# A decoder layer on one core: entries of the SwiGLU layers with other token operands first, and their tensor operations on VectorE alone

## The chip, the core and the metric

The kernel runs on one core of one Trainium2 chip. The metric is the device time of one execution in microseconds (us), and the numbers compared are medians over runs. The core has a matmul engine (TensorE, "PE" in the profile), a vector engine (VectorE, "DVE"), an activation engine (ScalarE, "ACT"), GpSimd ("POOL"), and SyncE ("SP"), which here issues the DMA transfers. Every engine works through its own queue in the order in which its instructions were emitted.

## The reference

One layer of a hybrid decoder trunk, for 1024 tokens of width 1024 in float32:

```python
x = x + 1/2 * SwiGLU_1(RMSNorm(x))
x = x + W_out [ DilatedAttn(heads 0..7) || Retention(heads 0..3) ]
x = x + CrossAttn(RMSNorm(x), RMSNorm(mem))   # 4 heads, 256 memory tokens
x = x + 1/2 * SwiGLU_2(RMSNorm(x))
final RMSNorm
```

A SwiGLU is `silu(x @ Wg) * (x @ Wu) @ Wout` with a hidden width of 2816, and its weights stand in DRAM as float32.

## The kernel before

Each float32 operand of a large matmul is written as a high part (`whi`, `hi...`, rounded by ACT) and a low part (`wlo`, `lo...`, the rest, subtracted by DVE or POOL), and three matmuls high x high, high x low and low x high stand for one. `split` does this for weights: a copy on ACT, L215, then a subtraction, L217, in one of four pairs of buffers.

**The SwiGLU's first half** is `ffn_in`. It goes over the hidden columns in 11 groups (p = 0 to 10). A group computes its gate and up columns by seven products instead of eight (a Strassen scheme on 2x2 blocks: gate and up by the two halves of the 1024 features, and these by the two halves of the 1024 tokens); a product multiplies one of seven token operands with one of seven weight operands. The token operands B11, T1, T2, B21, T3, B22, T4 are made once for a SwiGLU by `make_t`: `minus` (L427) makes differences of normed and transposed tokens, `parts` makes the high part on ACT (L417) and the low part on DVE or POOL (L419), in two halves. The weight operands W[1] to W[7] are made anew in each group: four loads `raw` (`load_raw`, L222), the sums s1 to s4 (`comb`, L497; s1 and s2 and s4 stand in one `hn` buffer, s3 in a `raw` buffer), and a `split` each. W[5] is the split of s1, W[6] of s2, W[7] of s3, W[3] of s4; W[1], W[2] and W[4] are splits of loads. A product is 24 matmuls of 512 columns (L522). In each group the products follow as 1 (B11), 5 (T1), 6 (T2), 2 (B21), 7 (T3), 3 (B22), 4 (T4).

Behind the products: three copies from PSUM on ACT (L533), three additions on DVE (L536), two silu on ACT (L539), then `h2` (L568), `e1` (L551), `h1` (L572), which reads T4's product from PSUM, and `e2`, `e3`, `e4` (L551, halves of 128x512). `h1`, `e1` to `e4` and `h2` are the operands of the second half `ffn_out`; four stores put them in DRAM. Also in each group but the first, `w_sums` (L471) loads 256 rows of the second half's weights, makes four differences of 128x512, and stores them; the last group does this twice.

**The order of all engines** comes from a planner, `Flow.run`: every operation is a node with a duration by a formula, dependences and buffers; the planner places one node after another at its planned time and writes each engine's instructions in that order. An operation on two SBUF tensors may go on DVE or POOL, and takes the engine with the earlier planned end, where `n.bias` is added first; `fl.bias` is empty in the kernel before. Once written, the order on an engine is fixed, and an instruction whose input is late holds all that stand behind it there.

**Around the SwiGLUs.** The first stage makes the keys and values of `mem` in eight blocks j (matmuls L256 to L258, weights `w_ckv`). In block j one tile of 128 rows of x is loaded, normed (the square on ACT L350, L352 on POOL, L353 on DVE) and, one block later, transposed by eight matmuls (L300) into the raw tokens of `make_t`. The eighth tile is transposed after the last block, and then the first SwiGLU starts. The second SwiGLU starts behind the cross attention's output, which is two sweeps (`sweep`) over four halves; in the last one the eight tiles of x come out one after another, are added (L1353), normed and transposed. The buffers for token operands are opened in two lots: T_EARLY (B11, T1, T2) and T_LATE (B21, T3, B22, T4). Before the second SwiGLU, `to_ffn2` closes the cross attention's buffers behind that sweep and opens both lots.

Of the kernel before, what the change touches and what calls it, by code (L numbers as in the profile page):

```python
# [152 lines left out]
def kernel(ctx: ExitStack, tc: tile.TileContext, x, mem,  # L153
# [246 lines left out]
    def make_t(R, done, early, late):  # L402

        def q(j, c):
            return [R[j, c, h] for h in range(2)]
# [4 lines left out]
        def parts(name, src, deps, give=None):  # L410
            out = []
            for h in range(2):
                ts = slice(h * 256, h * 256 + 256)
# [3 lines left out]
                a = N("ACT", cost_act(1024), lambda v=v, ts=ts: act.activation(TT[name][0][:, :, ts], v(), AF.Copy),  # L417
                      deps=deps[h] + [early if name in T_EARLY else late])
                out.append(N(("DVE", "POOL"), (cost_dve(1024), cost_pool(1024)), lambda e, v=v, ts=ts: two[e].tensor_tensor(  # L419
                    TT[name][1][:, :, ts], v(), f32(TT[name][0][:, :, ts]), op=OP.subtract), deps=[a],  # L420
                    give=[src[h]] if give else []))
# [4 lines left out]
        def minus(dst, a, b, deps):
            return [[N(("DVE", "POOL"), (cost_dve(1024), cost_pool(1024)), lambda e, h=h: two[e].tensor_tensor(  # L427
                dst[h].v, a[h].v, b[h].v, op=OP.subtract), deps=deps[h])] for h in range(2)]
# [53 lines left out]
    def ffn_in(wi, hids, wo, wts):  # L482
        stored = {}
        for p in range(NF // 2):
# [2 lines left out]
            if p == NK - 1:  # L487
                w_sums(wo, wts, p, stored)
            raws = {}
            for u, j in ((0, 0), (1, 0), (1, 1), (0, 1)):  # L490
                raws[u, j] = load_raw(rows(wi, j * 512, u * DFF + 2 * p * P, 4, 256), 4)
            (a11, l11), (a21, l21), (a22, l22), (a12, l12) = (raws[k] for k in ((0, 0), (1, 0), (1, 1), (0, 1)))
            sm = Hold(s_hb)
# [3 lines left out]
                         lambda e: two[e].tensor_tensor(dst.v, a.v, b.v, op=op), deps=deps, need=need, give=give)  # L497
# [34 lines left out]
            def copy(dst, b, deps):  # L532
                return N("ACT", cost_act(S), lambda: act.activation(dst.v, flat(b), AF.Copy), deps=deps, need=[dst])  # L533
# [17 lines left out]
                return N(("DVE", "POOL"), (cost_dve(512), cost_pool(512)), lambda e: two[e].tensor_tensor(  # L551
                    o[0](o[1]), a[0](a[1]), b[0](b[1]), op=op), deps=deps, need=need)
# [1 line left out]
            m1 = prod(1, x, "B11", True)
            a = copy(ta, x, [m1])
            z = Hold(pairs)
            m5 = prod(5, z, "T1", True)
            d = copy(td, z, [m5])
            m6 = prod(6, x, "T2", False, [a])
            b_ = copy(tb, x, [m6])  # L560
            y = Hold(pairs)
            m2 = prod(2, y, "B21", True)
            g1 = silu(ta, [add(ta, y, [m2, a], [y])])
            m7 = prod(7, x, "T3", False, [b_])
            u2 = add(td, x, [m7, d])
            m3 = prod(3, z, "B22", False, [d])
            g2 = silu(tb, [add(tb, z, [m3, b_], [z])])
# [139 lines left out]
    mp = open_pool(mctx, "memp")  # L710
# [28 lines left out]
    g1 = load_gain(norm_ffn1[0])  # L739
    R = raw_quarters()  # L740
    rdone = {}
    for j in range(8):
# [17 lines left out]
        kv_stored.append(dma(256, lambda kv=kv, j=j: sp.dma_start(  # L760
            kvs[j * 256:j * 256 + 256].rearrange("(i p) m -> p i m", p=P), kv.v), deps=[c], give=[kv]))
        hb, sc = norm_scale(lambda x_=x_: x_.v, [xl], g1, None, [x_])

        def later(j=j, hb=hb, sc=sc):
            b = Hold(pairs)
            tr = transposes(lambda k: hb.v[:, k * P:(k + 1) * P], [sc], b, give=[hb])
            rdone[j] = to_raw(R, tr, b, j)
        Later.add(1, later)
# [781 lines left out]
```

## Time and profile before

| | |
|---|---|
| median of three runs | 2161.68 us (2161.47 to 2163.49) |
| profiled execution, its own time | 2164.8 us |
| span from first to last instruction | 2163.0 us |
| mean granted TensorE clock | 0.984 |
| first stage | 0 to 75.6 us |
| first SwiGLU, first half | 75.62 to 509.55 us |
| second SwiGLU, first half | 1503.29 to 1941.76 us |

How to read the rows that are shown further on. A row of the timeline has the start in us, the time taken in us, the engine, the line, the operation, what it writes and reads, and the number of instructions that the row joins; in brackets stand the idle time of the engine ahead of it and the instruction that ended it. A row of the table by stretches has the stretch, its length, then the busy time of PE, PE's weight loads, DVE, ACT and POOL, then the granted TensorE clock, the DMA share and GB/s. The chain is the work that ended last, followed back from the end.

### The profile page before, as it was taken

The page shows a single profiled execution, that of the slowest core. Times are in us where ns is not written, and L with a number is a line of the kernel's source. Part 1 is how long each engine was busy: PE and PEld are TensorE (multiplying, and loading weights), DVE is VectorE, ACT ScalarE, POOL GpSimd, SP SyncE. Part 2 cuts the span into 40 slices and gives each one's busy share as a digit, 9 for nine tenths or more (in the row PEclk, how much of TensorE's full clock was granted, in tenths as well). Part 3 has the DMA queues.
Part 4 walks back from the last instruction along what each step waited for, and adds up shares of the span by engine and source line. Part 5 has one row for each costly group of instructions (what it writes and reads, how often), then busy time and mean ns, then how long its engine had stood idle before and what let it go on. Part 6 is the DMA issues. An engine that isn't in the chain of part 4 may idle for free.

```text
span 2163.0 us, 25267 instructions
## 1 busy us (share of the span) xinstructions
PE 2084.8 (96%) x9854; PEld 1724.0 (80%) x9854; DVE 1170.8 (54%) x1351; ACT 808.6 (37%) x1138; POOL 491.5 (23%) x341
## 2 busy tenths in 40 slices
PE   7899999999999999998999999998899999999997
PEld 7678888888888788887677788886688888888886
DVE  6956556565447420304896334525855656474464
ACT  5523323234335211114777423304332323333342
POOL 2533342340003100201220001003533233230031
PEclk9999999999999999998999999998999999999999
DMA  8344435457666542226743911112253544558554
GB/s 299 92 161 152 165 132 175 161 205 259 212 194 214 196 115 88 90 106 188 217 120 113 338 40 49 49 49 98 81 185 138 175 159 152 185 187 290 193 196 148
DMA packets 205991, 344.08 MB, mean 159 GB/s; under 512 B 12464, under 2 KB 100656, under 8 KB 205616
## 3 DMA queue, kind: packets, MB, share of 16 engines
q1 hardware_dynamic: 205872, 342.48, 46.9%
q8 instruction: 77, 1.26, 0.2%
q14 instruction: 42, 0.34, 0.0%
HBM read 239.14 MB, written 103.28 MB: 158 GB/s over the span
## 4 chain that ended last, share of the span: by engine, by line
PE 89%; DVE 5%; DMA 2%; issue 1%; ACT 1%; POOL 1%; SPq 0%; POOLq 0%; DVEq 0%; ACTq 0%
PE banks L522 37%; PE banks L630 19%; PE banks L258 9%; PE banks L257 9%; PE banks L256 9%; PE banks L300 2%; PE banks L1113 1%; PE banks L1094 1%; DVE loT L419 1%; DVE loB L419 1%; DMA tqk<-qs 1%; DVE wlo L217 1%; DVE hn L353 1%; PE banks L1057 0%; DVE hn L427 0%
## 5 line engine op out<-in xcount | busy, mean ns | idle before, releaser
L217 DVE TENSOR_TENSOR wlo<-raw,whi 128x1024 fp32r<-128x1024 f32 x159 | 218.2, 1392 | 363.1 <-ACT whi L215 360.0
L215 ACT ACTIVATE whi<-raw 128x1024 fp32r<-128x1024 f32 x168 | 175.2, 1055 | 327.2 <-issue 187.7
L630 PE MATMUL banks<-whi,hH 128*128 128x512 f32 x616 | 240.2, 390 | 0.7 <-DVE hn L648 0.7
L630 PE MATMUL banks<-wlo,hH 128*128 128x512 f32 x616 | 239.7, 389 | 0.0
L630 PE MATMUL banks<-whi,hL 128*128 128x512 f32 x616 | 239.7, 389 | 0.0
L522 PE MATMUL banks<-hiT,whi 128*128 128x512 f32 x704 | 219.6, 394 | 6.2 <-ACT hn L533 6.2
L522 PE MATMUL banks<-loT,whi 128*128 128x512 f32 x704 | 219.1, 393 | 6.5 <-DVE loT L419 6.5
L522 PE MATMUL banks<-hiT,wlo 128*128 128x512 f32 x704 | 218.6, 392 | 0.0
L256 PE MATMUL banks<-whi,aH 128*128 128x512 f32 x512 | 200.9, 392 | 0.0
L258 PE MATMUL banks<-whi,aL 128*128 128x512 f32 x512 | 199.3, 389 | 0.0
L257 PE MATMUL banks<-wlo,aH 128*128 128x512 f32 x512 | 199.3, 389 | 0.0
L536 DVE TENSOR_TENSOR hn<-banks,hn 128x1024 f32<-128x1024 f32 x66 | 80.8, 1224 | 194.2 <-PE banks L522 194.2
L522 PE MATMUL banks<-loB,whi 128*128 128x512 f32 x528 | 165.3, 395 | 7.8 <-DVE loB L419 7.8
L619 DVE TENSOR_TENSOR wlo<-raw,whi 128x1024 fp32r<-128x1024 f32 (+1 forms) x80 | 98.2, 1227 | 126.5 <-ACT whi L617 126.4
L522 PE MATMUL banks<-hiB,whi 128*128 128x512 f32 x528 | 165.0, 394 | 1.6 <-ACT hiB L417 1.6
L617 ACT ACTIVATE whi<-raw 128x1024 fp32r<-128x1024 f32 x84 | 83.1, 989 | 222.3 <-PE banks L630 189.6
L522 PE MATMUL banks<-hiB,wlo 128*128 128x512 f32 x528 | 164.0, 392 | 0.0
L522 PEld LDWEIGHTS banks<-loT,whi 128*128 128x128 f32 x704 | 133.6, 190 | 35.3 <-DVE loT L419 7.3
L522 PEld LDWEIGHTS banks<-hiT,whi 128*128 128x128 f32 x704 | 133.4, 190 | 35.2 <-ACT hn L533 7.5
L522 PEld LDWEIGHTS banks<-hiT,wlo 128*128 128x128 f32 x704 | 133.3, 189 | 28.1
L630 PEld LDWEIGHTS banks<-whi,hH 128*128 128x128 f32 x616 | 115.6, 188 | 25.4 <-issue 1.1
L630 PEld LDWEIGHTS banks<-whi,hL 128*128 128x128 f32 x616 | 115.6, 188 | 24.0
(174 smaller groups left out, 3827.4 us busy)
## 6 DMA issues: line engine op xcount, KB each, us to landing
raw<-in_w_ffn_in_dram SPq DMA_DIRECT2D x88, 512.0 KB, 5.5
raw<-hids SPq DMA_DIRECT2D x70, 512.0 KB, 5.4
hids<-hn SPq DMA_DIRECT2D x66, 512.0 KB, 2.8
hn<-in_w_ffn_out_dram SPq DMA_DIRECT2D x44, 512.0 KB, 4.4
wts<-hn SPq DMA_DIRECT2D x44, 512.0 KB, 2.7
raw<-wts SPq DMA_DIRECT2D x40, 512.0 KB, 3.9
raw<-in_w_ffn_out_dram SPq DMA_DIRECT2D x30, 512.0 KB, 4.0
raw<-in_w_in_dram SPq DMA_DIRECT2D x24, 512.0 KB, 6.2
```

What stands on the lines that cost most here:

```text
L215: a = N("ACT", cost_act(1024), lambda: act.activation(hold.v[0], src(), AF.Copy), deps=deps, need=[hold], prio=prio)
L217: lambda e: two[e].tensor_tensor(hold.v[1], src(), f32(hold.v[0]), op=OP.subtract), deps=[a], give=give, prio=prio)
L256: pe.matmul(o, sh, mh, start=start, stop=False)
L257: pe.matmul(o, sh, ml, start=False, stop=False)
L258: pe.matmul(o, sl, mh, start=False, stop=stop)
L300: pe.transpose(need.v[:, k // 4, (k % 4) * P:(k % 4 + 1) * P], src(k), ident)
L419: out.append(N(("DVE", "POOL"), (cost_dve(1024), cost_pool(1024)), lambda e, v=v, ts=ts: two[e].tensor_tensor(TT[name][1][:, :, ts], v(), ...
L522: pe.matmul(b.v[:, f], s_[:, k, f * P:f * P + P], m_[:, k], start=start and k == 0 and n == 0, stop=k == 3 and n == 2, skip_group_check=True)
L536: return N("DVE", cost_dve(S), lambda: dve.tensor_tensor(dst.v, flat(b), dst.v, op=OP.add), deps=deps, give=give)
L617: h = N("ACT", cost_act(n), lambda raw=raw, hold=hold, n=n: act.activation(hold.v[0][:, 0:n], raw.v[:, 0:n], AF.Copy), deps=[ld], need=[hold])
L619: l = N(("DVE", "POOL"), (cost_dve(n), cost_pool(n)), lambda e, raw=raw, hold=hold, n=n: two[e].tensor_tensor(hold.v[1][:, 0:n], raw.v[:, ...
L630: pe.matmul(bs[t // 2].v[:, t % 2], ah.v[s_][:, ts], wh.v[w_][:, ws], start=start and k + q == 0 and i == 0, stop=k + q == NK - 1 and i == ...
```

## The change

Five things are different.

1. `fl.bias` is `{"POOL": 1000.0}` from the start to the end of the first SwiGLU, and again for the second. With 1000 us added to the planned end on POOL, every operation on two tensors there goes on DVE. DVE has 1458 instructions instead of 1276 in its queue's listing, POOL 139 instead of 324. The middle of the program keeps its rule.
2. T_EARLY is B11, B21, T1, and `make_t` makes B21 ahead of T1.
3. Group 0 of each SwiGLU takes the products as 1, 2, 5, 6, 3, 7, 4, loads its weights and makes its splits to suit. The other groups keep theirs.
4. In the first stage the tiles of x are loaded by a table, X_AT: two in block 1 and two in block 3, none in the last two, so that all transposes stand ahead of block 6.
5. The last sweep takes its halves as (1, 0), and behind its first half `to_early` closes some of the cross attention's buffers and opens T_EARLY, so that B11 and B21 can be made during the second half; `to_ffn2` opens only T_LATE.

```diff
+DVE_ONLY = {"POOL": 1000.0}
...
-    T_EARLY, T_LATE = ("B11", "T1", "T2"), ("B21", "T3", "B22", "T4")
+    T_EARLY, T_LATE = ("B11", "B21", "T1"), ("T2", "T3", "B22", "T4")
...
         p1 = parts("B11", r11, has[0])
+        p2 = parts("B21", r21, has[0])
...
-        p2 = parts("B21", r21, has[0])
...
-            for u, j in ((0, 0), (1, 0), (1, 1), (0, 1)):
+            order = (1, 5, 6, 2, 7, 3, 4) if p else (1, 2, 5, 6, 3, 7, 4)
+            for u, j in ((0, 0), (1, 0), (1, 1), (0, 1)) if p else ((0, 0), (0, 1), (1, 0), (1, 1)):
...
-    def sweep(ws, evac, korder=(0, 1)):
+    def sweep(ws, evac, korder=(0, 1), middle=None):
...
+            if kg == 0 and middle:
+                middle()
...
+    fl.bias = DVE_ONLY
     open_t(ectx, T_EARLY, "right")
...
+    X_AT = ((0,), (1, 2), (3,), (4, 5), (6,), (7,), (), ())
...
-        x_, xl = ld_rows(x, j)
+        xin = [(i, *ld_rows(x, i)) for i in X_AT[j]]
...
     fl.base = 200.0
+    fl.bias = {}
...
-    sweep(sweep_w(vos, 512, deps=v_stored), add_x(1, fin_cross))
+    early = []
+    def to_early():
         bctx.close()
         kctx.close()
         open_t(ectx, T_EARLY, "right")
+    sweep(sweep_w(vos, 512, (1, 0), v_stored), add_x(1, fin_cross), (1, 0),
+          lambda: early.append(N("SP", 0.0, to_early, deps=t_users + c_users + v_users)))
...
     fl.base = 600.0
+    fl.bias = DVE_ONLY
...
-    make_t(R, rdone, sw, sw)
+    make_t(R, rdone, early[0], sw)
```

In the listings below the number behind an underscore names a buffer. Lines of the kernel after are those of before plus 1 ahead of `ffn_in`; within it L471 becomes L472, L497 L499, L522 L536, L533 L547, L551 L565, L568 L590, L572 L594.

**Between group 1 and group 2 of the first SwiGLU.** DVE before, from `h2` of group 1 on; the last two rows are s3 and W[6] of group 2:

```order
L568 TENSOR_TENSOR hn7_101<-hn7_101,hn3_97 128x1024
L551 TENSOR_TENSOR hn3_97<-hn7_101 128x512
L572 TENSOR_TENSOR hn6_100<-hn6_100,banks_85 128x1024
L551 TENSOR_TENSOR hn3_97<-hn3_97,hn6_100 128x512
L551 TENSOR_TENSOR hn7_101<-hn6_100,hn7_101 128x512
L551 TENSOR_TENSOR hn4_98<-hn6_100,hn3_97 128x512
L497 TENSOR_TENSOR raw3_108<-raw0_105,raw3_108 128x1024
L217 TENSOR_TENSOR wlo0_113<-hn5_99,whi0_109 128x1024
```

POOL before, over the same stretch: W[5] and s2 of group 1, then s1 of group 2 (`hn5_99`), the four differences of `w_sums`, and W[5] of group 2 (`wlo2_115<-hn5_99`):

```order
L217 TENSOR_TENSOR wlo0_113<-hn8_102,whi0_109 128x1024
L497 TENSOR_TENSOR hn8_102<-hn8_102,raw0_105 128x1024
L497 TENSOR_TENSOR hn5_99<-raw3_108,raw2_107 128x1024
L471 TENSOR_TENSOR hn0_94<-hn0_94 128x512
L471 TENSOR_TENSOR hn0_94<-hn9_103,hn0_94 128x512
L471 TENSOR_TENSOR hn9_103<-hn9_103,hn0_94 128x512
L471 TENSOR_TENSOR hn9_103<-hn9_103 128x512
L217 TENSOR_TENSOR wlo2_115<-hn5_99,whi2_111 128x1024
```

Both queues run side by side, and POOL's holds nothing that reads group 1's T4. DVE after, over the same stretch:

```order
L590 TENSOR_TENSOR hn6_100<-hn6_100,hn7_101 128x1024
L565 TENSOR_TENSOR hn7_101<-hn6_100 128x512
L594 TENSOR_TENSOR hn3_97<-hn3_97,banks_85 128x1024
L565 TENSOR_TENSOR hn7_101<-hn7_101,hn3_97 128x512
L565 TENSOR_TENSOR hn6_100<-hn3_97,hn6_100 128x512
L565 TENSOR_TENSOR hn9_103<-hn3_97,hn7_101 128x512
L472 TENSOR_TENSOR hn1_95<-hn1_95 128x512
L472 TENSOR_TENSOR hn1_95<-hn2_96,hn1_95 128x512
L472 TENSOR_TENSOR hn2_96<-hn2_96,hn1_95 128x512
L472 TENSOR_TENSOR hn2_96<-hn2_96 128x512
L499 TENSOR_TENSOR hn5_99<-raw1_106,raw3_108 128x1024
L218 TENSOR_TENSOR wlo3_116<-hn5_99,whi3_112 128x1024
```

The four differences (L472), s1 of group 2 (L499) and its W[5] (the last row) now stand in DVE's queue behind `h1` (L594) and `e2` to `e4` of group 1. ACT after, from the silus of group 1 (L553) on; `hn0_94` is the copy of group 2's product with B11, and the row behind it is the high part of group 2's W[5]:

```order
L553 ACTIVATE hn3_97<-hn3_97 128x1024
L553 ACTIVATE hn6_100<-hn6_100 128x1024
L547 ACTIVATE hn0_94<-banks_85 128x1024
L216 ACTIVATE whi3_112<-hn5_99 128x1024
L216 ACTIVATE whi0_109<-hn5_99 128x1024
L216 ACTIVATE whi1_110<-raw2_107 128x1024
L216 ACTIVATE whi2_111<-raw1_106 128x1024
```

PE after, from the last rows of group 2's product with B11 on, with what each instruction waits for; T1's first matmuls wait for ACT, the high part of W[5], and its fifth for DVE, the low part:

```order
L536 MATMUL banks_85<-hiB11_120,whi2_111 128x512 x2
L536 MATMUL banks_85<-loB11_121,whi2_111 128x512 x2
L536 MATMUL banks_85<-hiB11_120,wlo2_115 128x512 x2
L536 MATMUL banks_85<-hiT1_124,whi3_112 128x512 [waits Activation_49]
L536 MATMUL banks_85<-hiT1_124,whi3_112 128x512
L536 MATMUL banks_85<-loT1_125,whi3_112 128x512 x2
L536 MATMUL banks_85<-hiT1_124,wlo3_116 128x512 [waits DVE_49]
L536 MATMUL banks_85<-hiT1_124,wlo3_116 128x512
```

No instruction of PE changed its place here; what its waits name changed from POOL to DVE.

**At the start of the first SwiGLU.** PE before, from the last matmuls of the eighth block on:

```order
L256 MATMUL banks_85<-mH_134,whi3_112 128x256
L257 MATMUL banks_85<-mL_135,whi3_112 128x256
L258 MATMUL banks_85<-mH_134,wlo3_116 128x256
L300 MATMUL banks_85<-ident_86,hn5_99 128x128 x8
L522 MATMUL banks_85<-hiB11_120,whi0_109 128x512 x2
L522 MATMUL banks_85<-loB11_121,whi0_109 128x512 x2
L522 MATMUL banks_85<-hiB11_120,wlo0_113 128x512 x2
```

PE after:

```order
L259 MATMUL banks_85<-mH_134,wlo3_116 128x256
L257 MATMUL banks_85<-mH_134,whi3_112 128x256
L258 MATMUL banks_85<-mL_135,whi3_112 128x256
L259 MATMUL banks_85<-mH_134,wlo3_116 128x256
L536 MATMUL banks_85<-hiB11_120,whi0_109 128x512 x2
L536 MATMUL banks_85<-loB11_121,whi0_109 128x512 x2
L536 MATMUL banks_85<-hiB11_120,wlo0_113 128x512 x2
```

The eight transposes ahead of the first product are gone from there; the last of them now stand ahead of block 6.

**At the start of the second SwiGLU.** PE before, from the last matmuls of the sweep on; `hn3_97` is the normed eighth tile:

```order
L257 MATMUL banks_85<-wlo3_116,aH1_7471 128x512
L258 MATMUL banks_85<-whi3_112,aL1_7472 128x512
L300 MATMUL banks_85<-ident_86,hn7_101 128x128 x8
L300 MATMUL banks_85<-ident_86,hn8_102 128x128 x8
L300 MATMUL banks_85<-ident_86,hn3_97 128x128 x8
L522 MATMUL banks_85<-hiB11_9547,whi0_109 128x512 x2
L522 MATMUL banks_85<-loB11_9548,whi0_109 128x512 x2
```

PE after:

```order
L258 MATMUL banks_85<-wlo2_115,aH0_7832 128x512
L259 MATMUL banks_85<-whi2_111,aL0_7833 128x512
L301 MATMUL banks_85<-ident_86,hn4_98 128x128 x8
L301 MATMUL banks_85<-ident_86,hn7_101 128x128 x8
L301 MATMUL banks_85<-ident_86,hn8_102 128x128 x8
L301 MATMUL banks_85<-ident_86,hn3_97 128x128 x8
L536 MATMUL banks_85<-hiB11_9331,whi0_109 128x512 x2
L536 MATMUL banks_85<-loB11_9332,whi0_109 128x512 x2
```

The transposes of the last four tiles now follow the sweep as one piece. DVE before, from the norm of the eighth tile on (L353), with W[5] of group 0 (`wlo2_115`) right behind it:

```order
L353 SCALAR_TENSOR_TENSOR hn3_97<-xt_7837,stat_t_89,gain_93 128x1024
L217 TENSOR_TENSOR wlo2_115<-hn8_102,whi2_111 128x1024
L497 TENSOR_TENSOR hn8_102<-hn8_102,raw0_105 128x1024
L419 TENSOR_TENSOR loB11_9548<-hn1_95,hiB11_9547 128x4x256
L497 TENSOR_TENSOR raw3_108<-raw0_105,raw3_108 128x1024
L419 TENSOR_TENSOR loB11_9548<-hn5_99,hiB11_9547 128x4x256
L427 TENSOR_TENSOR hn5_99<-hn4_98,hn5_99 128x1024
L419 TENSOR_TENSOR loB21_9557<-hn2_96,hiB21_9556 128x4x256
```

DVE after, up to W[5] of group 0 (`wlo1_114`); the norm of the eighth tile is six rows above the first row shown:

```order
L428 TENSOR_TENSOR hn4_98<-hn7_101,hn4_98 128x1024
L420 TENSOR_TENSOR loT1_9336<-hn5_99,hiT1_9335 128x4x256
L428 TENSOR_TENSOR hn5_99<-hn7_101,hn5_99 128x1024
L420 TENSOR_TENSOR loT2_9567<-hn1_95,hiT2_9566 128x4x256
L420 TENSOR_TENSOR loT3_9569<-hn9_103,hiT3_9568 128x4x256
L420 TENSOR_TENSOR loT2_9567<-hn5_99,hiT2_9566 128x4x256
L420 TENSOR_TENSOR loT3_9569<-hn4_98,hiT3_9568 128x4x256
L420 TENSOR_TENSOR loB22_9571<-hn0_94,hiB22_9570 128x4x256
L420 TENSOR_TENSOR loB22_9571<-hn7_101,hiB22_9570 128x4x256
L428 TENSOR_TENSOR hn1_95<-hn2_96,hn1_95 128x1024
L428 TENSOR_TENSOR hn5_99<-hn6_100,hn5_99 128x1024
L218 TENSOR_TENSOR wlo1_114<-hn8_102,whi1_110 128x1024
```

W[5] of group 0 now stands behind all the differences, and behind the low parts of all token operands but T4.

More of the change, by code (lines that the diff above doesn't have):

```diff
@@ L499, in ffn_in, with split2 @@
             W[1] = split(lambda a11=a11: a11.v, [l11])
+            def split2(a12=a12, l12=l12):
+                W[2] = split(lambda: a12.v, [l12])
+            if not p:
+                split2()
             s1 = comb(sm, a21, a22, OP.add, [l21, l22], need=[sm])
@@ L503, in ffn_in, with split7 @@
             W[6] = split(lambda sm=sm: sm.v, [s2])
-            W[2] = split(lambda a12=a12: a12.v, [l12])
+            if p:
+                split2()
             s3 = comb(a21, a11, a21, OP.subtract, [s1, s2, W[1][1]], give=[a11])
-            W[7] = split(lambda a21=a21: a21.v, [s3], [a21])
+            def split7(a21=a21, s3=s3):
+                W[7] = split(lambda: a21.v, [s3], [a21])
+            if p:
+                split7()
             s4 = comb(sm, a12, sm, OP.subtract, [W[6][1], W[2][1]], give=[a12])
             W[3] = split(lambda sm=sm: sm.v, [s4], [sm])
+            if not p:
+                split7()
             W[4] = split(lambda a22=a22: a22.v, [l22, s1], [a22])
@@ L553, in ffn_in @@
             x = Hold(pairs)
[L554 to L567, printed above, removed]
+            y = z = None
+            for i in order[:-1]:
+                if i == 1:
+                    m1 = prod(1, x, "B11", True)
+                    a = copy(ta, x, [m1])
+                elif i == 5:
+                    z = Hold(pairs)
+                    m5 = prod(5, z, "T1", True)
+                    d = copy(td, z, [m5])
+                elif i == 6:
+                    m6 = prod(6, x, "T2", False, [a])
+                    b_ = copy(tb, x, [m6])
+                elif i == 2:
+                    y = Hold(pairs)
+                    m2 = prod(2, y, "B21", True)
+                    g1 = silu(ta, [add(ta, y, [m2, a], [y])])
+                elif i == 7:
+                    m7 = prod(7, x, "T3", False, [b_])
+                    u2 = add(td, x, [m7, d])
+                else:
+                    m3 = prod(3, z, "B22", False, [d])
+                    g2 = silu(tb, [add(tb, z, [m3, b_], [z])])
             h2 = N(("DVE", "POOL"), (cost_dve(S), cost_pool(S)), lambda e, td=td, tb=tb: two[e].tensor_tensor(
@@ L761, with later @@
             kvs[j * 256:j * 256 + 256].rearrange("(i p) m -> p i m", p=P), kv.v), deps=[c], give=[kv]))
[L762 to L768, printed above, removed]
+        for i, x_, xl in xin:
+            hb, sc = norm_scale(lambda x_=x_: x_.v, [xl], g1, None, [x_])
+            def later(i=i, hb=hb, sc=sc):
+                b = Hold(pairs)
+                tr = transposes(lambda k: hb.v[:, k * P:(k + 1) * P], [sc], b, give=[hb])
+                rdone[i] = to_raw(R, tr, b, i)
+            Later.add(1, later)
         fl.groups = []
@@ L1435, in fin_cross @@
         Later.add(3, later)
-    sweep(sweep_w(vos, 512, deps=v_stored), add_x(1, fin_cross))
+    early = []
+    def to_early():
+        bctx.close()
+        kctx.close()
+        open_t(ectx, T_EARLY, "right")
+    sweep(sweep_w(vos, 512, (1, 0), v_stored), add_x(1, fin_cross), (1, 0),
+          lambda: early.append(N("SP", 0.0, to_early, deps=t_users + c_users + v_users)))
     Later.drain()
     fl.base = 600.0
+    fl.bias = DVE_ONLY
     fl.groups = []
@@ L1446, in to_ffn2 @@
         octx.close()
-        bctx.close()
-        kctx.close()
-        open_t(ectx, T_EARLY, "right")
         open_t(lctx, T_LATE, "left")
     sw = N("SP", 0.0, to_ffn2, deps=v_users + t_users + c_users)
-    make_t(R, rdone, sw, sw)
+    make_t(R, rdone, early[0], sw)
     stored = ffn_in(w_ffn2_in, hids2, w_ffn2_out, wts2)
```

## The prediction

> **What bounds the kernel now.** I read the page's totals and its chain first, then the table by stretches, then PE's own timeline where it waits.
>
> ```profile
> PE 2084.8 (96%) x9854; PEld 1724.0 (80%) x9854; DVE 1170.8 (54%) x1351; ACT 808.6 (37%) x1138; POOL 491.5 (23%) x341
> PE 89%; DVE 5%; DMA 2%; issue 1%; ACT 1%; POOL 1%; SPq 0%; POOLq 0%; DVEq 0%; ACTq 0%
> ...
> 75.00:131.00 56.00, 47.14 (x183) 37.71 (x182) 43.76 (x26) 23.76 (x25) 28.40 (x12) 0.89 0.27 89
> 131.00:500.00 369.00, 369.00 (x1629) 305.56 (x1628) 218.72 (x169) 122.09 (x122) 124.28 (x68) 1.00 0.47 167
> 1495.00:1560.00 65.00, 46.97 (x177) 36.37 (x175) 54.17 (x32) 30.47 (x33) 38.00 (x17) 0.84 0.24 81
> ```
>
> PE is the bound. In the steady part of the first SwiGLU (the second reads alike) it is busy in all of 369.00 us and has the full clock; what can be won lies in the two entries (89% and 84% of the clock). What can be lost lies in the steady part, where nothing is to be won.
>
> ```profile
> 74.00 1.97 PE L300 MATMUL banks<-ident,hn 128*128 128x128 f32 x8 [4.58 <-DVE hn L353]
> 75.62 1.20 PE L522 MATMUL banks<-hiB,whi 128*128 128x512 f32 x2
> 84.48 0.73 PE L522 MATMUL banks<-loT,whi 128*128 128x512 f32 x2 [1.88 <-DVE loT L419]
> 94.47 1.22 PE L522 MATMUL banks<-loB,whi 128*128 128x512 f32 x2 [4.25 <-DVE loB L419]
> 112.21 1.22 PE L522 MATMUL banks<-hiT,whi 128*128 128x512 f32 x2 [2.73 <-ACT hn L533]
> 281.07 0.61 PE L522 MATMUL banks<-hiB,whi 128*128 128x512 f32 x2
> 286.51 0.61 PE L522 MATMUL banks<-hiT,whi 128*128 128x512 f32 x2
> 509.55 0.39 PE L630 MATMUL banks<-whi,hH 128*128 128x512 f32 x1
> ...
> 1500.15 1.51 PE L300 MATMUL banks<-ident,hn 128*128 128x128 f32 x8 [4.71 <-DVE hn L353]
> 1503.29 1.22 PE L522 MATMUL banks<-hiB,whi 128*128 128x512 f32 x2 [1.63 <-ACT hiB L417]
> 1508.11 1.22 PE L522 MATMUL banks<-loB,whi 128*128 128x512 f32 x2 [3.60 <-DVE loB L419]
> 1521.37 1.22 PE L522 MATMUL banks<-loT,whi 128*128 128x512 f32 x2 [4.62 <-DVE loT L419]
> 1531.27 1.13 PE L522 MATMUL banks<-hiT,whi 128*128 128x512 f32 x2 [3.11 <-ACT hn L533]
> 1538.46 0.62 PE L522 MATMUL banks<-hiB,whi 128*128 128x512 f32 x2
> 1544.47 0.74 PE L522 MATMUL banks<-hiT,whi 128*128 128x512 f32 x2 [0.36 <-ACT hn L533]
> 1941.76 0.39 PE L630 MATMUL banks<-whi,hH 128*128 128x512 f32 x1
> ```
>
> A product takes 286.51 - 281.07 = 5.44 us, 77 of them 418.9. From 75.62 to 509.55 it took 433.9, so 15.0 are lost: 8.9 in three waits, 6.2 to a lower clock behind them. From 1503.29 to 1941.76 it took 438.5, 19.6 lost: 11.7 in waits, 7.9 to the clock. With the waits just ahead (4.58; 4.71 and 1.63) entry 1 holds 19.6 us and entry 2 25.9. The clock's price: 6.2 + 7.9 = 14.1 over seven waits of 2.7 or more (the pair 4.71 and 1.63 as one) is 2.0 for each. Single ones: one product from 1531.27 to 1538.46 took 7.19, 1.75 too many; from 112.21 on, the 72.5 products that were left (394.4) took 397.3, 2.95 too many. The wait of 2.73 was short and still slowed what followed (1.22 for two matmuls instead of 0.61).
>
> **The entries.** Early operands, an earlier x and no POOL work beside DVE aim at these 45.5 us. Beside POOL a full-size DVE operation took 3.30 instead of 1.21:
>
> ```profile
> 84.46 3.30 DVE L427 TENSOR_TENSOR hn<-hn,hn 128x1024 f32<-128x1024 f32 x1
> 83.37 3.30 POOL L497 TENSOR_TENSOR hn<-raw,hn 128x1024 f32<-128x1024 f32 x1 [1.16 <-DVE wlo L217]
> 248.06 1.21 DVE L497 TENSOR_TENSOR raw<-raw,raw 128x1024 f32<-128x1024 f32 x1
> 249.20 1.21 DVE L217 TENSOR_TENSOR wlo<-hn,whi 128x1024 fp32r<-128x1024 f32 x1
> 1498.82 1.28 DVE L353 SCALAR_TENSOR_TENSOR hn<-xt,stat_t,gain 128x1024 f32<-128x1024 f32 x1 [2.48 <-POOL stat_t L352]
> ```
>
> Entry 1: all transposes lie ahead of block 6, so two of the first stage's eight blocks, by its 75.6 us well over 10, cover B11, B21 and the first half of T1. DVE makes one full-size operation per 1.14 us (249.20 - 248.06); group 0 needs 14 low parts of tokens, 8 differences and 11 operations for weights, 33 or 37.6 us in all, against seven products of 5.44, 38.1, and those made during the blocks come off. Going down DVE's order at that pace against PE's, I find W[6] 1.8 early and only W[3] late, by 0.2. So I take 19 of 19.6. The loads of x go ahead of weight loads on SP; the block's weight that falls behind a store there is then issued about 24.1, behind the row of 23.74, and ACT reads that block's weights only from 30.23 on, so this costs nothing; if that cover were gone, the block would start late by what is missing, ahead of the operands that PE no longer waits for:
>
> ```profile
> 23.74 0.37 SPq L760 DMA_DIRECT2D kvs<-kvo  x1
> 30.23 2.00 ACT L215 ACTIVATE whi<-raw 128x1024 fp32r<-128x1024 f32 x2
> ```
>
> Entry 2: B11 waits as before for the eighth tile's norm, since the transposes stand ahead of it on PE. Of the 4.71 at most the 2.48 goes that the norm waited for POOL's statistics, since POOL has no sum of weights ahead of them any more; that leaves 2.2 to 4.7, and I take 3.5, the middle. Then W[5]'s low part stands 16 full-size operations behind that norm: 1.28 + 16 x 1.14 + 1.23 = 20.7 us after its start, where PE has 1.5 of transposes, B11 and B21 (10.9) and T1's first four matmuls (0.9), with the norm 14.6: a wait of 6. With 0.7 for W[6] and two slow starts (4.0) 14.2 of 25.9 remain, and 12 are won. Both entries: 31, between half of it and all 45.5. The re-ordered products of group 0 and its loads cost nothing by themselves: the same matmuls and bytes.
>
> **The steady part.** All 20 later groups change too. The rows of a group's end, and what POOL did beside it:
>
> ```profile
> 244.05 1.21 DVE L572 TENSOR_TENSOR hn<-hn,banks 128x1024 f32<-128x1024 f32 x1
> 245.29 1.65 DVE L551 TENSOR_TENSOR hn<-hn,hn 128x512 f32<-128x512 f32 x1
> 246.86 1.28 DVE L551 TENSOR_TENSOR hn<-hn,hn 128x512 f32<-128x512 f32 x2
> 252.60 1.21 DVE L497 TENSOR_TENSOR hn<-raw,hn 128x1024 f32<-128x1024 f32 x1
> 253.93 1.06 ACT L215 ACTIVATE whi<-hn 128x1024 fp32r<-128x1024 f32 x1 [2.51 <-DVE hn L497]
> 254.89 1.01 ACT L533 ACTIVATE hn<-banks 128x1024 f32<-128x1024 f32 x1
> 255.02 1.23 DVE L217 TENSOR_TENSOR wlo<-hn,whi 128x1024 fp32r<-128x1024 f32 x1 [1.21 <-ACT whi L215]
> ...
> 275.63 0.61 PE L522 MATMUL banks<-hiT,whi 128*128 128x512 f32 x2
> 275.83 1.22 DVE L536 TENSOR_TENSOR hn<-banks,hn 128x1024 f32<-128x1024 f32 x1 [4.21 <-PE banks L522]
> ...
> 259.41 2.40 POOL L497 TENSOR_TENSOR hn<-raw,raw 128x1024 f32<-128x1024 f32 x1 [13.03 <-DMA raw<-in_w_ffn_in_dram]
> 268.68 1.29 POOL L471 TENSOR_TENSOR hn<-hn 128x512 f32<-128x512 f32 x1 [6.87 <-DMA hn<-in_w_ffn_out_dram]
> 279.18 2.48 POOL L217 TENSOR_TENSOR wlo<-hn,whi 128x1024 fp32r<-128x1024 f32 x1 [4.95 <-ACT whi L215]
> ```
>
> Before, s1 was made at 259.41, `w_sums` from 268.68 and W[5] at 279.18, ready for T1 at 286.51, since POOL's queue did not wait for T4, which ends at 281.07. In the order after, they stand on DVE behind `h1`, which does. PE has only B11 between. From T4's end: `h1` starts at 0.20 (275.83 - 275.63); `e2` 1.24 later (245.29 - 244.05). Then seven halves, `e2` to `e4` and four differences: a step is 0.60 (248.06 - 246.86, halved), a duration 1.28 - 0.60 = 0.68, and where one reads the one before it, 0.71 with the 0.03 seen behind `h1`; four of 0.60 and three of 0.71 are 4.5. So s1 starts at 6.0. W[5]'s high part starts 1.33 behind such a start (253.93 - 252.60) and ends 1.06 later, at 8.4; its low part starts at 8.4 (255.02 - 252.60 = 2.42) and ends at 9.6. T1's first matmul needs the high part, its fifth the low one. PE, done with B11 at 5.44, waits 2.9, longer than the 2.73 that slowed it; four matmuls at the low clock take 1.8, so the low part is then nearly there. Price: 2.9 + 2.0 = 4.9, in eight groups 39.2. In group 1 half of B11 stands ahead of T4, so the cover is 2.7 shorter: 7.6. The last group has four differences more, 2.7: 7.6. Together 54.4, twice 108.8. What waits behind T1 on PE is everything; W[6] is ready by 13.2 (two steps of 1.14 and 1.23 behind W[5]), before T1 ends at 15.8, so there is no second wait.
>
> POOL's freed time gains nothing here. DVE has room (218.72 of 369, and POOL's 124.28 at half the time each is some 62 more): it is order, not load.
>
> **Sum.** 108.8 - 19 - 12 = +77.8. On the profiled execution's 2164.8 this gives 2242.6; that one is 3.1 above the median of 2161.7, from which I forecast 2239.5, say 2240. Ends: all steps 0.60 and a clock price of 1.75 make 97 and, with all entries won, +52 (2213); all steps 0.71, 2.95 and half of 31 make 137 - 15 = +122 (2283).
>
> **Rivals.**
> A second case keeps the waits but not the slow clock: a wait of 2.9 might often not be enough. Then T1 also waits 0.35 for the low part: 3.25 x 8 + 5.95 x 2 = 37.9, twice 75.8, less 31 to 45.5: +45 to +30, 2192 to 2207. Against it: the waits of 2.73 and 3.11 both slowed PE. [...]
>
> A third ends faster. The place in DVE's queue decides only if it makes W[5] late; if its high part were there by 5.44, the steady part stayed without a gap and only entries counted: 2131, down to 2116. For it: DVE's idle share, and halves of 1.65 beside POOL that become 0.68. [...] Against it: 0.68 is in my sum already, and ACT alone copies B11's product (1.01) ahead of W[5]'s high part (1.06): PE waits 2.1 there even if DVE is early.
>
> A fourth is no change: only this 2.1 in 20 places, 42, and no slow clock, against 45.5 won. Within 0.2% (4.3 us) is what a measurement here cannot tell from no change.
>
> A fifth is slower still: a second wait at T2 in each group, some 2 + 2.0 in 20 places, 80 more, 2320. It needs DVE another 2.7 late, as by loads of `w_sums`; those landed at 268.68, 12 before T4's end.
>
> **How the numbers follow.** The waits with the slow clock (2213 to 2283) 0.70; without it (2192 to 2207) 0.11; faster 0.08; no change 0.04; beyond 2283 0.07. The range 2192 to 2283 leaves out 0.19. Faster 0.08, same 0.04, slower 0.88.
>
> **What would show it.** PE waits at T1 once in each group but the first, released by ACT's high part, about 2.9, with the clock below 1.00 in the steady table; the timeline has s1 on DVE behind `h1`. Entry 1 nearly without waits; in entry 2 one of 3 to 4 before B11 and one near 6 in T1. I am wrong if the steady part shows no such waits, or if they are under 2 or over 4, or if the entries keep theirs.

## The result, and the profile after

The changed kernel takes 2240.94 us, the median of four runs (2239.99 to 2243.16), beside 2162.42 for the kernel before (four runs): a ratio of 1.0364, 95% interval 1.0346 to 1.0382. It is 78.5 us slower; 2240 had been forecast.

The page after, its totals and its chain:

```profile
PE 2114.7 (94%) x9854; PEld 1739.2 (78%) x9854; DVE 1199.2 (54%) x1531; ACT 815.1 (36%) x1143; POOL 122.3 (5%) x156
PE 83%; DVE 9%; issue 2%; DMA 2%; ACT 2%; POOL 1%; SPq 0%; POOLq 0%; DVEq 0%; ACTq 0%
```

POOL is nearly empty (491.5 us of work before), and DVE has no larger share than before: 54%. Its part of the chain rose from 5% to 9%. Averages over the whole span do not show the loss; the table by stretches does. Its columns are the stretch, its length, busy time and instructions of PE, PE's loads, DVE, ACT and POOL, then the granted clock:

```profile
70.00:131.00 61.00, 55.41 (x250) 45.93 (x249) 45.59 (x43) 26.73 (x29) 0.00 (x0) 0.94 0.32 113
131.00:500.00 369.00, 345.68 (x1468) 280.94 (x1467) 205.52 (x202) 103.79 (x102) 0.00 (x0) 0.97 0.40 141
1500.00:1560.00 60.00, 52.72 (x239) 43.52 (x238) 52.04 (x51) 33.94 (x46) 7.57 (x16) 0.89 0.21 82
1560.00:1970.00 410.00, 381.15 (x1606) 309.93 (x1605) 228.55 (x225) 119.09 (x117) 0.00 (x0) 0.96 0.40 143
```

In the steady part of the first SwiGLU PE did 1468 matmuls in 369 us, where it had done 1629: 161 x 0.2267 = 36.5 us lost in eight groups. DVE was busy for 205.52 of 369, less than before. PE's waits over the whole span, the two lines of the SwiGLUs (total, times, longest):

```profile
PE banks L536 <- ACT whi L216: 68.2, 20, 5.6
...
PE banks L536 <- DVE wlo L218: 4.1, 1, 4.1
```

Twenty waits for a weight's high part. One of them on the three engines, from T4's end (242.60) on, and the start of T1 in the next two groups:

```profile
242.60 0.61 PE L536 MATMUL banks<-hiB,whi 128*128 128x512 f32 x2
...
251.07 0.73 PE L536 MATMUL banks<-hiT,whi 128*128 128x512 f32 x2 [2.87 <-ACT whi L216]
251.65 0.63 PE L536 MATMUL banks<-loT,whi 128*128 128x512 f32 x2
252.33 1.22 PE L536 MATMUL banks<-hiT,wlo 128*128 128x512 f32 x2
253.35 1.06 PE L536 MATMUL banks<-hiT,whi 128*128 128x512 f32 x2
...
294.26 0.73 PE L536 MATMUL banks<-hiT,whi 128*128 128x512 f32 x2 [2.87 <-ACT whi L216]
...
335.85 0.73 PE L536 MATMUL banks<-hiT,whi 128*128 128x512 f32 x2 [2.87 <-ACT whi L216]
...
242.80 1.22 DVE L594 TENSOR_TENSOR hn<-hn,banks 128x1024 f32<-128x1024 f32 x1 [1.14 <-PE banks L536]
244.06 1.90 DVE L565 TENSOR_TENSOR hn<-hn,hn 128x512 f32<-128x512 f32 x3
245.87 0.69 DVE L472 TENSOR_TENSOR hn<-hn 128x512 f32<-128x512 f32 x1
246.59 1.42 DVE L472 TENSOR_TENSOR hn<-hn,hn 128x512 f32<-128x512 f32 x2
248.04 0.69 DVE L472 TENSOR_TENSOR hn<-hn 128x512 f32<-128x512 f32 x1
248.65 1.22 DVE L499 TENSOR_TENSOR hn<-raw,raw 128x1024 f32<-128x1024 f32 x1
251.05 1.22 DVE L218 TENSOR_TENSOR wlo<-hn,whi 128x1024 fp32r<-128x1024 f32 x1 [1.18 <-ACT whi L216]
...
248.24 1.02 ACT L547 ACTIVATE hn<-banks 128x1024 f32<-128x1024 f32 x1 [8.56 <-PE banks L536]
249.96 1.06 ACT L216 ACTIVATE whi<-hn 128x1024 fp32r<-128x1024 f32 x1 [0.70 <-DVE hn L499]
```

DVE waits for T4 with `h1` (242.80), goes without a gap through `e2` to `e4` and the four differences, and reaches s1 at 248.65, 6.05 behind T4's end; ACT makes the high part, PE starts T1 at 251.07. From 252.33 on, 1.26 behind the end of the wait, eight matmuls take 3.51 us (to 255.84), where eight take 1.81 at full clock (0.2267 each); the first two of them take 1.22 instead of 0.61.

The two entries, by the first product's and the second half's first matmul, and by the waits between them in the second:

```profile
73.10 0.63 PE L536 MATMUL banks<-hiB,whi 128*128 128x512 f32 x2
544.71 0.39 PE L652 MATMUL banks<-whi,hH 128*128 128x512 f32 x1
...
1531.76 1.50 PE L301 MATMUL banks<-ident,hn 128*128 128x128 f32 x8 [2.30 <-DVE hn L354]
1534.09 1.97 PE L301 MATMUL banks<-ident,hn 128*128 128x128 f32 x8 [0.84 <-DVE hn L354]
1535.71 1.20 PE L536 MATMUL banks<-hiB,whi 128*128 128x512 f32 x2
1553.51 1.22 PE L536 MATMUL banks<-hiT,wlo 128*128 128x512 f32 x2 [4.14 <-DVE wlo L218]
2017.36 0.39 PE L652 MATMUL banks<-whi,hH 128*128 128x512 f32 x1
```

The first SwiGLU's first half starts 2.5 us earlier and has no wait in group 0; it takes 471.6 instead of 433.9. The second takes 481.7 instead of 438.5.

### The profile page after: what moved, and what is told of

Same layout as the page of the kernel before. It is cut to its first block, busy times and chain, and to the rows that moved or that the text cites. A ratio compares the mean times of both kernels' runs of the same rounds, so it can differ in the third digit from the quotient of the medians.

```text
span 2238.6 us, 25121 instructions
## 1 busy us (share of the span) xinstructions
PE 2114.7 (94%) x9854; PEld 1739.2 (78%) x9854; DVE 1199.2 (54%) x1531; ACT 815.1 (36%) x1143; POOL 122.3 (5%) x156
## 3 DMA queue, kind: packets, MB, share of 16 engines
q8 instruction: 77, 1.26, 0.2%
## 4 chain that ended last, share of the span: by engine, by line
PE 83%; DVE 9%; issue 2%; DMA 2%; ACT 2%; POOL 1%; SPq 0%; POOLq 0%; DVEq 0%; ACTq 0%
PE banks L536 34%; PE banks L652 18%; PE banks L259 9%; PE banks L258 9%; PE banks L257 9%; DVE hn L472 2%; PE banks L301 1%; DVE hn L499 1%; DVE hn L594 1%; ACT whi L216 1%; PE banks L1141 1%; PE banks L1122 1%; DMA hn<-kvs 1%; DVE hn L565 1%; DVE wlo L218 1%
## 5 line engine op out<-in xcount | busy, mean ns | idle before, releaser
L218 DVE TENSOR_TENSOR wlo<-raw,whi 128x1024 fp32r<-128x1024 f32 x163 | 195.6, 1221 | 341.5 <-ACT whi L216 340.5
L536 PE MATMUL banks<-hiT,whi 128*128 128x512 f32 x704 | 231.9, 412 | 68.2 <-ACT whi L216 68.2
L536 PE MATMUL banks<-hiT,wlo 128*128 128x512 f32 x704 | 230.1, 409 | 4.9 <-DVE wlo L218 4.1
L536 PE MATMUL banks<-loT,whi 128*128 128x512 f32 x704 | 226.4, 404 | 0.0
L536 PEld LDWEIGHTS banks<-hiT,whi 128*128 128x128 f32 x704 | 139.7, 201 | 105.6 <-ACT whi L216 76.6
L536 PEld LDWEIGHTS banks<-hiT,wlo 128*128 128x128 f32 x704 | 138.3, 198 | 39.2 <-DVE wlo L218 10.1
L536 PE MATMUL banks<-hiB,whi 128*128 128x512 f32 x528 | 163.4, 391 | 0.0
L536 PE MATMUL banks<-loB,whi 128*128 128x512 f32 x528 | 163.0, 390 | 0.0
L536 PE MATMUL banks<-hiB,wlo 128*128 128x512 f32 x528 | 163.0, 390 | 0.0
L536 PEld LDWEIGHTS banks<-loT,whi 128*128 128x128 f32 x704 | 139.0, 197 | 30.8
L641 DVE TENSOR_TENSOR wlo<-raw,whi 128x1024 fp32r<-128x1024 f32 x84 | 95.2, 1133 | 125.8 <-ACT whi L639 125.8
L547 ACT ACTIVATE hn<-banks 128x1024 f32<-128x1024 f32 x66 | 67.4, 1020 | 225.6 <-PE banks L536 225.6
```

The lines of the kernel that those rows point to most:

```text
L218: lambda e: two[e].tensor_tensor(hold.v[1], src(), f32(hold.v[0]), op=OP.subtract), deps=[a], give=give, prio=prio)
L536: pe.matmul(b.v[:, f], s_[:, k, f * P:f * P + P], m_[:, k], start=start and k == 0 and n == 0, stop=k == 3 and n == 2, skip_group_check=True)
L641: l = N(("DVE", "POOL"), (cost_dve(n), cost_pool(n)), lambda e, raw=raw, hold=hold, n=n: two[e].tensor_tensor(hold.v[1][:, 0:n], raw.v[:, ...
```

## The experiments

All times are medians; the kernel before took 2161.2 to 2162.6 beside them. The first half of a SwiGLU is 77 products of 5.44, 418.9 us, where PE never waits; its length in each profile shows where the time went.

| kernel | us | ratio to before, 95% | first half of SwiGLU 1 | of SwiGLU 2 |
|---|---|---|---|---|
| before | 2162.42 | | 433.93 | 438.47 |
| changed | 2240.94 | 1.0346 to 1.0382 | 471.61 | 481.65 |
| pool_steady | 2132.27 | 0.9844 to 0.9874 | 418.91 | 427.49 |
| te_last | 2132.19 | 0.9842 to 0.9875 | 418.91 | 427.54 |
| before_dve_steady | 2260.38 | 1.0436 to 1.0468 | 480.13 | 489.21 |
| warm | 2216.76 | 1.0238 to 1.0269 | 462.08 | 470.72 |
| wsums_pool | 2153.91 | 0.9953 to 0.9979 | 429.22 | 437.89 |
| order_all | 2175.07 | 1.0047 to 1.0079 | 442.04 | 448.45 |
| no_bias | 2145.42 | 0.9910 to 0.9940 | 423.33 | 431.67 |
| pool_w5 | 2126.71 | 0.9824 to 0.9853 | 418.91 | 420.52 |
| act_floor | 2190.05 | 1.0110 to 1.0140 | 448.55 | 455.41 |
| te_w5 | 2131.25 | 0.9835 to 0.9868 | 418.91 | 424.41 |

**pool_steady: the rule on POOL for the entries and group 0 alone.**

```diff
         for p in range(NF // 2):
+            fl.bias = {} if p else DVE_ONLY
...
+        fl.bias = DVE_ONLY
         return stored
```

> The changed kernel, but from group 1 of each SwiGLU on the operations on two tensors may go on POOL again, as before. Theory (the place of s1, W[5] and the differences in DVE's queue makes the steady waits): no waits at T1 in the steady part, clock 1.00 there, and only the gain of the entries is left: 2162.4 - 30 = 2132. Rival (the new product order, the early operands or the moved loads make the waits): waits at T1 stay, 2235 or so.

2132.27. The first SwiGLU has no wait left, 418.91 us. So the rest of the change does not make the steady waits by itself; they need the rule on POOL.

**te_last: everything on DVE, in another order.** The `hn` buffers are given out in the order in which the program asks for them. `te`, the buffer of `e4`, is asked for ahead of those of the next group's `w_sums` and s1, and is taken when `e4` is placed. As long as s1 stood on POOL it could be placed late and still get an early time there; on DVE it falls behind `h1`. The edit asks for `te` last; `nxt` holds the next group's three, two of `w_sums` and `sm`, the buffer of s1:

```diff
-                w_sums(wo, wts, p - 1, stored)
+                w_sums(wo, wts, p - 1, stored, nxt[:2])
...
-            sm = Hold(s_hb)
+            sm = nxt[2] if p else Hold(s_hb)
...
+            if p < NK - 1:
+                nxt = [Hold(s_hb) for _ in range(3)]
             te = Hold(s_hb)
```

> The changed kernel with everything still on DVE alone; only the queue for the hn buffers is changed, so that the buffer of e4 is asked for behind those of the next group's w_sums and s1. In the order s1 and W[5] then stand ahead of h1. Theory (order, not load): no waits at T1, about 2132 to 2140. Rival (DVE's load): the same number of DVE operations as the changed kernel, so the same 2241.

2132.19, the same as with POOL. Its table and the rows at a group's end:

```profile
131.00:500.00 369.00, 369.00 (x1629) 305.56 (x1628) 237.54 (x236) 122.93 (x120) 0.00 (x0) 1.00 0.49 167
...
225.75 0.61 PE L536 MATMUL banks<-hiB,whi 128*128 128x512 f32 x2
231.19 0.61 PE L536 MATMUL banks<-hiT,whi 128*128 128x512 f32 x2
...
225.95 1.22 DVE L594 TENSOR_TENSOR hn<-hn,banks 128x1024 f32<-128x1024 f32 x1 [1.14 <-PE banks L536]
227.20 1.89 DVE L565 TENSOR_TENSOR hn<-hn,hn 128x512 f32<-128x512 f32 x3
229.01 1.22 DVE L218 TENSOR_TENSOR wlo<-raw,whi 128x1024 fp32r<-128x1024 f32 x1
```

DVE is busier (237.54) and nobody waits: T1 follows B11 after 5.44. Behind `h1` (L594) stand no differences and no s1 any more. The rival of DVE's load falls, and the loss is one of order.

**before_dve_steady: the rule added to the kernel before, in groups 1 to 10.**

```diff
         for p in range(NF // 2):
+            fl.bias = DVE_ONLY if p else {}
```

> The kernel before, with DVE alone only in groups 1 to 10 of each SwiGLU. Theory: the twenty waits of 2.9 and 5.6 at T1 with their slow starts, 105 us, come back on top of the old entries: 2162.4 + 105 = 2267. Rival (the waits come from the rest of the change): 2162.

2260.38: the rule alone brings the waits, without the rest of the change. The first halves grow by 46.2 and 50.7, 97 in all, 8 less than expected; in this order of products no half of B11 stands ahead of T4 in group 1, so its wait is 2.87 instead of 5.6, which is 5.4 of the 8 (2.7 in each SwiGLU).

**warm: matmuls in place of the wait.** T1's PSUM gets twelve extra matmuls of B11 ahead of its own, which overwrite them:

```diff
+                        if i == 5 and p and not q:
+                            for n in range(12):
+                                pe.matmul(b.v[:, n % 2], TT["B11"][0][:, 0, 0:P], TT["B11"][0][:, n // 2 % 4],
+                                          start=True, stop=True, skip_group_check=True)
```

> The changed kernel with twelve extra matmuls of 512 columns ahead of T1 in each group but the first (their results are overwritten by T1), so that PE works 2.7 us of the wait of 2.9. Theory (each wait also costs a slow clock, 1.7 to 2.0): 16 of 20 slow starts are gone, the waits of 5.6 keep 2.9 each: 2241 - 28 = about 2213. Rival (the loss lies in the waits alone): no change, 2241. In both the steady waits at T1 shrink to 0.2 and 2.9.

2216.76, 24 us faster than the changed kernel for more work. The profile's row of the extra matmuls and those behind it:

```profile
245.99 2.88 PE L533 MATMUL banks<-hiB 128*128 128x512 f32 x12
249.02 0.72 PE L539 MATMUL banks<-hiT,whi 128*128 128x512 f32 x2
249.59 0.63 PE L539 MATMUL banks<-loT,whi 128*128 128x512 f32 x2
...
131.00:500.00 369.00, 365.73 (x1593) 297.38 (x1592) 213.48 (x214) 105.97 (x104) 0.00 (x0) 1.00 0.42 148
```

The clock stays at 1.00 in this stretch and no matmul behind is slow. The waits of 5.6 in groups 1 and 10 keep 2.87 each, and behind all four of them the clock was 0.79 to 0.81 in the next 8 us. The slow clock is a cost by itself, beside the wait.

**wsums_pool: the differences alone back on POOL.**

```diff
+        keep, fl.bias = fl.bias, {}
         t1 = minus((lo, a), (hi, a), (lo, a), [l[0]])
...
+        fl.bias = keep
```

> The changed kernel, but the four differences of w_sums may go on POOL; s1 and W[5] stay on DVE behind h1 and e2 to e4. If DVE's queue alone sets the wait, the chain is 2.7 shorter: the waits at T1 fall from 2.87 to about 0.2, in groups 1 and 10 as well, and the time to some 2140. If ACT's queue is a second floor (the copy of B11's product stands ahead of W[5]'s high part there): after the changed kernel's rows the high part can start 0.72 earlier and no more, so 20 like waits of 2.15, released by ACT, and 0.35 for the low part: 2132 + 50 = 2182 if 2.15 is too short to slow the clock, 2132 + 20 x 4.05 = 2213 if it isn't.

2153.91, between the two. The listed waits are gone but for one of 2.8 in group 1 of each SwiGLU, which is its 5.6 less the 2.7; behind the first of them the clock did not fall (1.00 from 70 to 131 us). In the steady stretch there are 1599 matmuls, 30 or 6.8 us fewer than 1629, in gaps too short to be listed. The stretch, and the start of T1 in two groups that follow each other:

```profile
131.00:500.00 369.00, 367.44 (x1599) 298.49 (x1598) 207.96 (x192) 120.48 (x118) 56.96 (x40) 1.00 0.46 162
...
157.52 0.73 PE L538 MATMUL banks<-hiT,whi 128*128 128x512 f32 x2
...
196.35 0.74 PE L538 MATMUL banks<-hiT,whi 128*128 128x512 f32 x2
```

A group takes 38.83 where seven products take 38.08: 0.75 more, of which 0.27 stands ahead of T1 and the rest ahead of its fifth matmul, which needs the low part. Ten times this and the 2.8 are the 10.3 that the first half takes over 418.9. So a chain shorter by 2.7 takes the wait nearly away, as DVE's queue alone had it. On ACT's floor the run says nothing: the planner put W[5]'s high part ahead of the copy there (234.09 and 235.13 in one group).

**act_floor: that floor by itself**, on pool_steady, with s1 early on POOL:

```diff
                     a = copy(ta, x, [m1])
+                    if p:
+                        w5 = W[5][1].deps[0]
+                        w5.deps.append(a)
+                        w5.wait += 1
+                        a.users.append(w5)
```

> pool_steady (no steady waits, 2132), with one dependence added in groups 1 to 10: the high part of W[5] on ACT also waits for the copy of B11's product, so that ACT has the changed kernel's order while s1 is early on POOL. The fourth rival's floor: by the changed kernel's rows (B11 ends 248.20, copy 1.02, high part 1.06) T1 waits 2.15 for ACT in all 20 groups and 0.3 for the low part on DVE; 2132 + 49 = 2181 if a wait of 2.15 doesn't slow the clock, 2216 if it slows it each time (1.88 did not in the kernel before, 2.73 did). If ACT's order has no price: 2132.

2190.05. Twenty waits of 2.06 to 2.12 in place of none, released by ACT; the first one, two from the middle, and the stretches of 8 us behind the first two:

```profile
118.47:126.47 8.00, 8.00 (x28) 6.51 (x29) 7.92 (x7) 3.64 (x4) 0.00 (x0) 0.79 0.62 228
242.04:250.04 8.00, 7.95 (x34) 6.25 (x35) 7.91 (x7) 3.99 (x4) 0.00 (x0) 1.00 0.30 94
...
118.47 1.22 PE L537 MATMUL banks<-hiT,whi 128*128 128x512 f32 x2 [2.12 <-ACT whi L216]
...
242.04 0.74 PE L537 MATMUL banks<-hiT,whi 128*128 128x512 f32 x2 [2.06 <-ACT whi L216]
...
405.21 1.22 PE L537 MATMUL banks<-hiT,whi 128*128 128x512 f32 x2 [2.06 <-ACT whi L216]
```

The floor is real: ACT's order alone costs 58 us here, 41.3 of them in these waits. The clock is below 1.00 behind 3 of the 20. So if ACT had kept that order, 58 of the 107 us would have stayed even with s1 early on DVE. In te_last ACT did not keep it: there W[5]'s high part (214.67) also stands ahead of the copy of B11's product (231.95).

**order_all: B21 ahead of T1 in all groups.** `order = (1, 2, 5, 6, 3, 7, 4)` for every p, with its loads and splits.

> The changed kernel with all groups in group 0's order of products, so that B21 too stands between T4 and T1: 10.9 us of cover instead of 5.44, for the same operations on DVE. In the order the addition of B21's product now stands between s1 and W[5]'s low part. Theory: high part in time, low part at 10.88 + 0.2 + 1.2 + 1.2 = 13.5 behind T4's end, T1's fifth matmul could start at 11.8: waits of 1.75, released by DVE, too short to slow the clock: 2132 + 35 = 2167 (2201 if they slow it). Rival (not the distance from h1 to T1): 2241.

2175.07. In this run nine matmuls of the second half (2.04) stand between the last two products of each first half; the lengths in the table leave them out (436.60 + 5.44 and 443.01 + 5.44 from the second half's first matmul). W[5]'s high part comes nearly in time, and the wait moved to its low part. In the last group of each SwiGLU, with its four differences more, the high part is late:

```profile
241.23 0.74 PE L530 MATMUL banks<-hiT,whi 128*128 128x512 f32 x2 [0.15 <-ACT whi L216]
243.58 0.73 PE L530 MATMUL banks<-hiT,wlo 128*128 128x512 f32 x2 [1.14 <-DVE wlo L218]
...
483.90 1.22 PE L530 MATMUL banks<-hiT,whi 128*128 128x512 f32 x2 [2.93 <-ACT whi L216]
```

Eighteen groups wait some 1.15 for the low part (1.75 expected), and the clock behind these waits was 1.00. The two waits of 2.93 are followed by 0.63 and 0.79 in 8 us. With twice the cover the loss of the first halves falls from 106.9 to 44.1 (23.1 over 418.9, and 21.0 over pool_steady's second). That is 9 more than the 35 expected: a common group takes 39.98 from T1 to T1, 1.9 over 38.08 with the gaps that are not listed, and the last group of each SwiGLU loses 6.0 and 3.9. For the same operations on DVE the cover between T4 and T1 is what counts.

**no_bias: the change without the rule on POOL.** `DVE_ONLY = {}`.

> The changed kernel without the rule that keeps operations off POOL: only the early operands, the new first group and the moved loads are left. No waits in the steady part. If work beside POOL is what makes the entries slow, several microseconds of their 30 are given back, DVE rows of 3.3 stand in the entries: 2137 to 2147. Rival (the rule is worth nothing in the entries): 2132.

2145.42, 13 us slower than pool_steady and 16 faster than the kernel before that ran beside it (2161.16). In the first entry DVE's operations are stretched again where POOL works beside them:

```profile
83.56 9.05 DVE L420 TENSOR_TENSOR loT<-hn,hiT 128x1024 fp32r<-128x1024 f32 x4
84.86 6.66 POOL L428 TENSOR_TENSOR hn<-hn,hn 128x1024 f32<-128x1024 f32 x2 [5.96 <-DVE loT L420]
...
101.64 0.80 PE L536 MATMUL banks<-hiB,whi 128*128 128x512 f32 x2 [1.90 <-ACT whi L216]
```

Four operations took 9.05, where they take 4.62 with no work on POOL beside them (at 77.33 in the changed kernel). By the ratios of the two runs, some 16 of the 30 that the entries gain are the earlier operands, the new order and the moved loads, and some 14 the rule on POOL. 4.6 and two POOL operations of 2.40 (the one at 259.41 in the kernel before) make 9.4, near the 9.05; that is an estimate, and the rows do not show what makes both slower.

**pool_w5 and te_w5: the last wait.** On pool_steady and te_last, the sums and splits of W[5], W[6] and W[3] of the second SwiGLU's group 0 get `prio=-1`, so that they go ahead of other operations that are ready.

> pool_steady, and in the second SwiGLU's group 0 the sums and splits of W[5], W[6] and W[3] go ahead of the token operands that are needed later, by their rank in the planner. Theory: the one wait that is left in the entries, 4.5 at T1's low part, and its slow start of 1.7 to 3.4 are gone: 2132 - 7 = about 2125. Rival: DVE is then late with the token operands of T2, B22 or T3 and the wait only moves on: 2132.

> te_last (all on DVE, hn buffer of e4 asked for last) with the rank of W[5], W[6] and W[3] in the second SwiGLU's group 0 as in pool_w5. Theory: DVE alone is no loss once the order is mended, and the last wait of 5.0 in the entries goes: 2126, as pool_w5. Rival (DVE alone costs something by its load): 2132 or more.

pool_w5 takes 2126.71, the fastest of all by its median, though the intervals of the two overlap: the 4.5 are gone, and the first half of the second SwiGLU is 7.0 shorter. The slow start of 1.7 to 3.4 was an estimate, and no run shows that range: in pool_steady T1 and T2 took 18.15 there (1494.35 to 1512.50) where two products take 10.88, of which 4.52 is the wait and 2.75 the rest. te_w5 takes 2131.25, no clear gain on te_last: its wait of 5.0 is gone, but one of 2.36 for an addition on DVE stands at 1520.87 instead, where the differences of `w_sums` share DVE's queue. There the rival was right.

## Why the prediction was right, point by point

**The steady part.** Its sum was 108.8. Against pool_steady, which differs by these waits alone, the first halves are 52.7 and 54.2 longer: 106.9. Of these 68.2 are waits (2.87 sixteen times, 5.6 four times; 2.9 and 5.6 were forecast) and 38.7 the slow clock and smaller gaps, 1.9 for each wait (2.0 was forecast, all for the clock). Every step of the chain up to T1 came as worked out: `h1` 0.20 behind T4's end, s1 at 6.05 (6.0), the high part ended at 8.42 (8.4), the low part started at 8.45 (8.4).

That 1.9 is so near 2.0 is in part luck. The prediction let T1's first four matmuls run at the low clock (1.8), so that the fifth would hardly wait for the low part. They took 1.26 (251.07 to 252.33), and the fifth did wait. From 294.26 to 335.85, with the clock at 1.00, a group took 41.59 where seven products take 38.08: 3.51, which is 0.64 more than the wait that is listed. Taken off for all 20, this leaves 25.9 for the clock, 1.5 behind each of the 17 waits that slowed it. The term for the clock was too large and the term for the low part, put at next to nothing, too small.

**The entries.** Entry 1 gained 2.5 ahead of its first product and 15.0 behind, 17.5 (19). Entry 2 gained 2.7 ahead (the span between the two first halves fell from 993.7 to 991.0) and 11.0 behind, 13.7 (12): the norm's wait was 3.1 (3.5), T1's 4.1 (6), W[6]'s did not come. Entry 1 came 1.5 short and entry 2 1.7 over, which cancel. 106.9 - 17.5 - 13.7 = 75.7, and the span grew by 75.6.

**The rivals.** The case without the slow clock fell: behind 17 of the 20 waits the clock was lower in the next 8 us. Three of these, and last one of the three others, in the table by stretches:

```profile
165.33:173.33 8.00, 7.93 (x27) 6.08 (x28) 7.92 (x7) 3.23 (x4) 0.00 (x0) 0.79 0.53 185
208.52:216.52 8.00, 8.00 (x29) 6.52 (x30) 7.91 (x7) 3.87 (x4) 0.00 (x0) 0.82 0.51 184
509.17:517.17 8.00, 8.00 (x23) 6.39 (x24) 7.96 (x7) 2.95 (x3) 0.00 (x0) 0.63 0.50 176
294.26:302.26 8.00, 7.93 (x34) 6.26 (x35) 7.91 (x7) 3.99 (x4) 0.00 (x0) 1.00 0.53 185
```

The faster case fell with its condition, since s1 was late. Where W[5] comes in time, as in pool_steady and te_last, its 2131 did come (2132). The 2.1 that stood against it for ACT's order were 2.06 to 2.12 in act_floor, and cost more there (58) than the entries gain. A second wait in each group did not come. The sign "over 4" was worded too narrowly: four of the waits are 5.6, as the prediction's own sum has them.

**What the prediction did not know** is why s1 stood behind `h1`: it read it from the order. te_last shows the cause, a buffer asked for too early.

## What to carry to other kernels

Before an operation is moved to another engine, look at what stands ahead of it in that engine's queue, and count from that one's input to the reader: an engine that is half idle is no cover when its queue waits for the engine that it is to feed. A gain by less contention in one stage is no reason for a rule in the next; here the same rule won some 14 us at the entries and lost 107 behind them. Where a planner orders by time, a buffer that is given out in the order of asking can bind operations that have nothing else in common.

## What the runs showed of the hardware

In these runs the longer waits slowed PE more often: in the changed kernel the clock was lower behind 13 of 16 waits of 2.87 and all four of 5.6, in act_floor behind 3 of 20 waits of 2.06 to 2.12. Length alone does not decide: beside the 13 of 16, all four waits of 2.87 in warm and both of 2.93 in order_all were followed by slow matmuls, and the first one of 2.8 in wsums_pool was not (clock 1.00 from 70 to 131 us); what tells equal waits apart stays open. Nor does the low clock begin at a fixed moment: at 405.21 in act_floor the first matmuls are slow at once (1.22 for two instead of 0.61), at 251.07 in the changed kernel only those 1.26 later. Where it came in the changed kernel, the clock over the next 8 us was 0.77 to 0.82 fifteen times and 0.63 twice. Twelve matmuls without use in the wait were worth 24 us: in warm the clock was 1.00 from 131 to 500 us, where it had been 0.97.
